# An expert layer of eight equal steps becomes four full experts beside four half-empty ones

## The chip, the core and the metric

The program runs on one core of a Trainium2 chip. The metric is the device time of one execution in microseconds (us); the kernel before takes 1585.5 us (median of three runs, 1585.26 to 1587.52).

## The reference, cut to what matters

Two decoder layers over 256 tokens of width 1024. Each has three token mixers, a merge and a LayerNorm; then layer 0 has a dense SwiGLU and layer 1, with which this case deals, eight experts of which each token takes two:

```
logits = x @ w_router                                   # 256 x 8
top_logit, top_idx = top_k(logits, 2); top_w = softmax(top_logit)
for each expert e, its tokens xs:
    y = (silu(xs @ w_gate[e]) * (xs @ w_up[e])) @ w_down[e]     # 1024 -> 2816 -> 1024
out[token] += top_w * y;   x = LayerNorm(alpha * x + out)
```

All is float32. The inputs are fixed (seed 0). The weights of the eight experts are 8 x 3 x 1024 x 2816 x 4 bytes = 276.8 MB and are read once.

## The kernel before

Every weight travels in units of 1 MB (128 partitions x 2048 float32), in the order in which `pack` laid them down. `fetch` (L166) has SyncE (SP) start the transfer of the next unit into the next of seven buffers of the expert layer (six `raw`, one `ga`); a buffer is free when both its halves have been split. `split` (L188) turns half a unit, 128x1024, into `hi` (rounded to fp32r, ScalarE, ACT, L196) and `lo` (the rest, VectorE, DVE, L198), in one of nine pairs of buffers. `mm3` (L206) then makes a product of nearly float32 precision from three TensorE (PE) matmuls: activation-high by hi, activation-high by lo, activation-low by hi (L208 to L210).

Expert layer (`moe`, L1031): a step is 256 of the 2816 inner columns of one expert, three units: two of gate and up, one of down. There are 8 experts x 11 = 88 steps, expert after expert in the order of memory. An expert has 128 slots; `gather` makes a one-hot matrix from the tokens' places and multiplies, so that the slots' activations stand as `xeh` (high) and `xel` (low), 128 columns each, for two experts at once. Per step, PE does 24 matmuls of 512 columns for gate and up into the PSUM tile `pa`, then ACT (Silu, L1093) and DVE (times up, L1094) make the hidden activation, PE transposes it (L1099), ACT and DVE split it into `hh` and `hl` (L1103, L1104), and PE does 12 matmuls for down, one step later (`pend`), into two tiles `Y`. After an expert's last step `scatter` splits Y, multiplies with the turned one-hots `oht` (L1056, L1057) and adds the weighted rows into the accumulator `ybc` (L221). `weights` (L963) makes the softmax weights and the fullest expert's count.

Should an expert have more than 128 tokens, `spill` (L1117) does the rest in a loop that reads all weights again, with addresses from a register; the trace shows only its test (TENSOR_LOAD of `mosti`, L1119).

A scheduler orders each engine's instructions, from the program's order and its own estimate of readiness; `issue_after` holds single ones back. Each engine executes its own list in order and waits on semaphores.

Of the kernel before, what the change touches and what calls it, by code (L numbers as in the profile page):

```python
# [21 lines left out]
T = 256  # L22
# [4 lines left out]
NE = 8  # L27
# [18 lines left out]
GA = 3  # L46
# [88 lines left out]
class Net:  # L135
# [29 lines left out]
    def fetch(self):  # L165
# [5 lines left out]
        w = self.A["wst"][self.unit]  # L171
# [742 lines left out]
    def route_consts(self):  # L914
# [12 lines left out]
        nc.vector.tensor_copy(self.identr, self.ident)  # L927
        self.sel = C.tile([128, 2, NE], F32, name="sel")
# [34 lines left out]
    def weights(self):  # L963
        nc, C = self.nc, self.cst
        ps = self.pa()
        for m in range(2):
            nc.tensor.matmul(ps[:, 0:NE], lhsT=self.ones, rhs=self.sel[:, m], start=m == 0, stop=m == 1)
        most = C.tile([128, 1], F32, name="most")
        nc.vector.tensor_reduce(most, ps[:, 0:NE], axis=AX.X, op=OP.max)
        self.most = C.tile([128, 1], I32, name="mosti")  # L970
        nc.vector.tensor_copy(self.most, most)
# [7 lines left out]
        for m in range(2):  # L979
            nc.vector.tensor_scalar(ex[:, m], ex[:, m], den[:, m:m + 1], None, op0=OP.mult)  # L980
            nc.vector.tensor_scalar(self.wt[:, m], self.oh8[:, m, 0], ex[:, m, 0:1], None, op0=OP.mult)
            self.stt(self.wt[:, m], self.oh8[:, m, 1], ex[:, m, 1:2], self.wt[:, m])
        self.dump("pos", self.pos)
        self.dump("wt", self.wt)

    def gather(self, es, W):
        nc = self.nc
        n = len(es)
        oh = W.tile([128, 2, n * 128], F32R, name="ohm", bufs=2)
        self.front = []  # L990
        for m in range(2):
            for i, e in enumerate(es):
                self.front.append(nc.vector.tensor_scalar(oh[:, m, i * 128:(i + 1) * 128], self.slot,
                                                          self.pos[:, m, e:e + 1], None, op0=OP.is_equal))
        xeh = [W.tile([128, 8, 128], F32R, name="xeh", bufs=3) for _ in es]
        xel = [W.tile([128, 8, 128], F32R, name="xel", bufs=3) for _ in es]
        for kp in range(4):
            ps = self.pa()
            for kk in range(2):
                k = 2 * kp + kk  # L1000
                s = slice(k * 128, (k + 1) * 128)
                o = ps[:, kk * 256:kk * 256 + n * 128]
                for m in range(2):
                    nc.tensor.matmul(o, lhsT=self.xkh[:, m, s], rhs=oh[:, m], start=m == 0, stop=False)  # L1004
                    nc.tensor.matmul(o, lhsT=self.xkl[:, m, s], rhs=oh[:, m], start=False, stop=m == 1)
            pv = ps.rearrange("p (k i t) -> p k i t", k=2, t=128)
            for i in range(n):
                q = slice(2 * kp, 2 * kp + 2)
                nc.scalar.copy(xeh[i][:, q], pv[:, :, i])
                self.front.append(nc.vector.tensor_sub(xel[i][:, q], pv[:, :, i], xeh[i][:, q]))  # L1010
            yield
        return [xeh, xel, oh]

    def finish(self, gen):
        while True:
            try:
                next(gen)
            except StopIteration as r:
                return r.value

    def turn(self, oh, W):
        nc = self.nc
        oht = W.tile([128, 2, T], F32R, name="oht", bufs=2)
        for i in range(2):
            ps = self.psA.tile([128, 512], F32R, name="pa")
            for m in range(2):
                nc.tensor.transpose(ps[:, m * 128:(m + 1) * 128], oh[:, m, i * 128:(i + 1) * 128], self.identr)
            nc.scalar.copy(oht[:, i], ps[:, 0:T])  # L1028
        return oht

    def moe(self, W):  # L1031
        nc = self.nc
        acc = self.macc
        got = coming = None
# [3 lines left out]
        pend = None  # L1038

        def down(j, hh, hl2, wd, Y, ns=(0, 1)):  # L1040
            for f in range(2):
                for n in ns:
                    s = slice(n * 512, (n + 1) * 512)
                    self.mm3(Y[n], hh[:, f], hl2[:, f], wd[f][0][:, s], wd[f][1][:, s], j == 0 and f == 0,
                             j == NJ - 1 and f == 1)

        def scatter(e, Y, oht, ns=(0, 1)):
            for n in ns:
# [3 lines left out]
                nc.scalar.copy(yh, Y[n])  # L1052
                nc.vector.tensor_sub(yl, Y[n], yh)
                for m in range(2):
                    ps = self.pb()
                    nc.tensor.matmul(ps, lhsT=oht[:, m * 128:(m + 1) * 128], rhs=yh, start=True, stop=False)  # L1056
                    nc.tensor.matmul(ps, lhsT=oht[:, m * 128:(m + 1) * 128], rhs=yl, start=False, stop=True)  # L1057
                    self.stt(acc[:, m, s], ps, self.wt[:, m, e:e + 1], acc[:, m, s])

        for e in range(NE):  # L1060
            if e % 2 == 0:
                got = self.finish(coming or self.gather((e, e + 1), W))
                coming = None
                if e == 0:
                    self.after(SPLITS[1], self.front[SPLITS[4]])
            Y = oht = None
            for j in range(NJ):
                if e == 0 and j == 1:
                    self.weights()
                    for m in range(2):  # L1070
                        nc.scalar.mul(acc[:, m], self.xt[m], ALPHA)
                if e % 2 and e < NE - 1 and GA <= j < GA + 4:
                    if coming is None:
                        coming = self.gather((e + 1, e + 2), W)
                    next(coming, None)
                if j == 2:
                    if e % 2 == 0:
                        got[2] = self.turn(got[2], W)
                    oht = got[2][:, e % 2]
                ps = self.pa()  # L1080
                for u in range(2):
                    raw = self.fetch()
                    for h in range(2):
                        hi, lo = self.split(raw[:, h * 1024:(h + 1) * 1024])
                        for kk in range(2):
                            k = 4 * u + 2 * h + kk
                            s = slice(kk * 512, (kk + 1) * 512)
                            self.mm3(ps, got[0][e % 2][:, k], got[1][e % 2][:, k], hi[:, s], lo[:, s], k == 0, k == 7)
                        if u == 1 and h == 0 and pend is not None and not (e == NE - 1 and j == NJ - 1):
                            pend()  # L1090
                            pend = None
                sg = W.tile([128, 256], F32, name="fs", bufs=2)
                nc.scalar.activation(sg, ps[:, 0:256], AF.Silu)  # L1093
                nc.vector.tensor_mul(sg, sg, ps[:, 256:512])  # L1094
                wd = list(self.halves())
                last = e == NE - 1 and j == NJ - 1
                pt = self.pb()
                for f in range(2):
                    nc.tensor.transpose(pt[:, f * 128:(f + 1) * 128], sg[:, f * 128:(f + 1) * 128], self.ident)  # L1099
                hh = W.tile([128, 2, 128], F32R, name="hh", bufs=2)  # L1100
                hl2 = W.tile([128, 2, 128], F32R, name="hl2", bufs=2)
                pv = pt[:, 0:256].rearrange("p (a t) -> p a t", a=2)
                nc.scalar.copy(hh, pv)  # L1103
                nc.vector.tensor_sub(hl2, pv, hh)  # L1104
                if Y is None:
                    Y = [self.pb(), self.pb()]
                before = pend

                def pend(ns=(0, 1), j=j, hh=hh, hl2=hl2, wd=wd, Y=Y, e=e, oht=oht):
                    down(j, hh, hl2, wd, Y, ns)  # L1110
                    if j == NJ - 1:
                        scatter(e, Y, oht, ns)
        for n in range(2):
            before((n,))
            pend((n,))

    def spill(self, W, base, after):  # L1117
# [10 lines left out]
        oht = W.tile([128, T], F32, name="oht", bufs=2)  # L1128
# [5 lines left out]
        with tc.If(most > 128):  # L1134
            nc.vector.tensor_scalar(pos, self.pos, -128.0, None, op0=OP.add)
# [142 lines left out]
```

## Time and profile before

| what | us |
|---|---|
| median of three runs | 1585.5 |
| the profiled execution | 1585.51 |
| its span (first to last instruction) | 1583.7 |
| PE / DVE / ACT busy in it | 1518.6 / 1275.1 / 931.7 |
| moved by DMA | 390.78 MB, 247 GB/s over the span |

The profile's page gives the busy time of each engine and cuts the span into 40 slices of 39.6 us; the expert layer is slices 20 to 40. The views of the trace used below are the busy time, granted clock and DMA rate of a stretch (windows), the instructions of a stretch in order of time (timeline), groups of equal instructions (lines), the events of one line of the source, and DMA issues.

### The profile page before, as it was taken

What the parts mean: (1) busy time and instruction counts of PE and PEld (TensorE: products, weight loads), DVE (VectorE), ACT (ScalarE), POOL (GpSimd) and SP (SyncE); (2) the same over time, 40 slices, a digit from 0 to 9 for tenths busy, and PEclk for the clock granted to TensorE, in tenths of its full rate; (3) what the DMA queues carried; (4) which work ended last, traced back from release to release, by engine and by line L of the source; (5) the groups of instructions that cost most, each with busy time, mean ns of one, the idle gap of its engine ahead of it and who ended that gap; (6) DMA issues with size and microseconds to landing.
All of it is one profiled execution on the core that took longest, in us unless ns stands there. A gap on an engine that the chain in (4) does not pass through costs nothing.

```text
span 1583.7 us, 23704 instructions
## 1 busy us (share of the span) xinstructions
PE 1518.6 (96%) x9398; PEld 1312.9 (83%) x9398; DVE 1275.1 (81%) x1717; ACT 931.7 (59%) x1235; POOL 44.4 (3%) x80
## 2 busy tenths in 40 slices
PE   7999999999999989999899999999999999999996
PEld 7989987999989989998788887887878878788784
DVE  6899588654556898578898988889898888888887
ACT  6433454544436433454777777777777767777673
POOL 1030000000000110000000000000000000000000
PEclk9999999999999999999899999999999999999998
DMA  6343246655414343245698898998989988899892
GB/s 230 110 160 131 94 152 234 218 208 186 173 67 147 107 146 121 94 179 233 263 353 349 329 351 307 369 359 317 349 318 366 363 331 332 321 360 363 330 372 76
DMA packets 55637, 390.78 MB, mean 247 GB/s; under 512 B 6192, under 2 KB 6192, under 8 KB 9568
## 3 DMA queue, kind: packets, MB, share of 16 engines
q1 hardware_dynamic: 53136, 381.18, 63.8%
q0 software_dynamic: 2096, 7.49, 1.4%
q8 instruction: 76, 1.25, 0.3%
q10 hardware_dynamic: 288, 0.52, 0.1%
q14 instruction: 41, 0.34, 0.1%
HBM read 387.08 MB, written 2.10 MB: 246 GB/s over the span
## 4 chain that ended last, share of the span: by engine, by line
PE 89%; DVE 7%; ACT 2%; issue 1%; DMA 0%; DVEq 0%; ACTq 0%; POOLq 0%
PE pa L208 19%; PE pa L209 19%; PE pa L210 19%; PE pb L208 7%; PE pb L210 7%; PE pb L209 7%; PE pb L585 2%; DVE lo L198 2%; PE pb L1099 1%; DVE ga L221 1%; ACT hi L196 1%; DVE M L523 1%; PE pa L1004 1%; DVE r L563 1%; DVE kk L540 1%
## 5 line engine op out<-in xcount | busy, mean ns | idle before, releaser
L198 DVE TENSOR_TENSOR lo<-raw,hi 128x1024 fp32r<-128x1024 f32 x648 | 771.2, 1223 | 149.4 <-ACT hi L196 146.9
L196 ACT CAST hi<-raw 128x1024 fp32r<-128x1024 f32 x648 | 655.8, 1050 | 281.7 <-PE pa L209 192.3
L208 PE MATMUL pa<-xTh,hi 128*128 128x256 f32 x1120 | 325.4, 291 | 7.3 <-ACT xTh L347 7.3
L210 PE MATMUL pa<-xTh,lo 128*128 128x256 f32 x1120 | 323.2, 289 | 7.0 <-DVE lo L198 6.8
L209 PE MATMUL pa<-xTl,hi 128*128 128x256 f32 x1120 | 321.7, 287 | 2.3 <-DVE xTl L348 2.0
L210 PE MATMUL pa<-hi,xel 128*128 128x512 f32 x704 | 283.1, 402 | 0.0
L208 PE MATMUL pa<-hi,xeh 128*128 128x512 f32 x704 | 279.9, 398 | 0.4 <-ACT oht L1028 0.4
L209 PE MATMUL pa<-lo,xeh 128*128 128x512 f32 x704 | 279.3, 397 | 0.0
L208 PEld LDWEIGHTS pa<-xTh,hi 128*128 128x128 f32 x1120 | 218.5, 195 | 12.0 <-ACT xTh L347 7.3
L210 PEld LDWEIGHTS pa<-xTh,lo 128*128 128x128 f32 x1120 | 218.6, 195 | 10.3 <-DVE lo L198 8.8
L209 PEld LDWEIGHTS pa<-xTl,hi 128*128 128x128 f32 x1120 | 218.6, 195 | 3.6 <-DVE xTl L348 2.3
L208 PE MATMUL pb<-hi,hh 128*128 128x512 f32 x440 | 174.4, 396 | 3.7 <-ACT hh L1103 3.7
L209 PE MATMUL pb<-lo,hh 128*128 128x512 f32 x440 | 173.4, 394 | 0.0
L210 PE MATMUL pb<-hi,hl 128*128 128x512 f32 x440 | 173.3, 395 | 0.0
L209 PEld LDWEIGHTS pa<-lo,xeh 128*128 128x128 f32 x704 | 132.6, 188 | 30.5
L210 PEld LDWEIGHTS pa<-hi,xel 128*128 128x128 f32 x704 | 132.6, 188 | 29.0
L208 PEld LDWEIGHTS pa<-hi,xeh 128*128 128x128 f32 x704 | 132.8, 189 | 28.6 <-ACT oht L1028 0.6
L1093 ACT ACTIVATE fs<-pa 128x256 f32<-128x256 f32 x88 | 33.9, 385 | 150.9 <-PE pa L210 150.9
L208 PEld LDWEIGHTS pb<-hi,hh 128*128 128x128 f32 x440 | 82.6, 188 | 24.2 <-ACT hh L1103 5.3
L210 PEld LDWEIGHTS pb<-hi,hl 128*128 128x128 f32 x440 | 82.6, 188 | 19.9 <-DVE hl L1104 0.2
L209 PEld LDWEIGHTS pb<-lo,hh 128*128 128x128 f32 x440 | 82.6, 188 | 19.3
L198 DVE TENSOR_TENSOR lo<-ga,hi 128x1024 fp32r<-128x1024 f32 x74 | 88.0, 1218 | 5.1 <-ACT hi L196 4.8
(329 smaller groups left out, 1538.4 us busy)
## 6 DMA issues: line engine op xcount, KB each, us to landing
raw<-in_wst SPq DMA_DIRECT2D x322, 1024.0 KB, 6.0
ga<-in_wst SPq DMA_DIRECT2D x37, 1024.0 KB, 6.8
raw<-in_wst SPq DMA_DIRECT2D x4, 512.0 KB, 5.8
xf<-in_xT SPq DMA_DIRECT2D x2, 512.0 KB, 5.5
raw<-in_lora SPq DMA_DIRECT2D x2, 512.0 KB, 5.7
kk<-in_lnp POOLq DMA_DIRECT2D x2, 512.0 KB, 3.9
v<-in_lnp POOLq DMA_DIRECT2D x2, 512.0 KB, 3.9
xsave<-ga POOLq DMA_DIRECT2D x2, 512.0 KB, 2.9
```

The source lines that it names most:

```text
L196: self.nc.scalar.copy(hi, src)
L198: self.nc.vector.tensor_sub(lo, src, hi)
L208: mm(out, lhsT=lh, rhs=rh, start=start, stop=False)
L209: mm(out, lhsT=lh, rhs=rl, start=False, stop=False)
L210: mm(out, lhsT=ll, rhs=rh, start=False, stop=stop)
L221: return self.nc.vector.scalar_tensor_tensor(out, a, s, b, op0=op0, op1=op1)
L523: nc.vector.tensor_mul(M[:, c % 2, c // 2, 4 * hb:4 * hb + 4], ps.rearrange("p (a t) -> p a t", a=4), self.mask[:, None, :].to_broadcast([ ...
L540: nc.vector.transpose(y[32 * q:32 * q + 32], src)
L563: self.inv = nc.vector.transpose(o, E[s].rearrange("p t b s -> p t (b s)"))
L585: ins = nc.tensor.matmul(ps[s, n * 64:(n + 1) * 64], lhsT=lhsT[s, 8 * b + n], rhs=rhs[s, 8 * b + n], start=True, stop=True)
L1004: nc.tensor.matmul(o, lhsT=self.xkh[:, m, s], rhs=oh[:, m], start=m == 0, stop=False)
L1093: nc.scalar.activation(sg, ps[:, 0:256], AF.Silu)
```

## The change

The number of tokens of each expert is now used. `rank` orders the experts by count on DVE: `order` (which expert has rank r), `posr` and `wtr` (places and weights by rank) and `cap` (128 for ranks 0 to 3, 64 for ranks 4 to 7); rank 0 is always expert 0 (its `tie` is 8192), whatever its count, the ranks behind it go by count. Ranks 0 to 3 ("big") are done as before, three passes on 128 slots. Ranks 4 to 7 ("small") have 64 slots: `xes` holds the 64 high and the 64 low columns side by side as one operand of 128, and `mm2` makes two matmuls, with hi and with lo, where `mm3` makes three. Gate and up then stand in two partial sums, one in rows 0 to 63 and one in 64 to 127; ACT copies them out (`gu`) and four matmuls with `fold` (two identities on top of each other) add and transpose them. The partial sums of down are added by the scatter, whose one-hots stand twice (`slot2`).

Steps alternate: two big ones, then small, big, small, big to the end, and the down product of a step stands two steps (`LAG`) behind its gate and up. Units of ranks 1 to 7 are read at an address in a register: SP loads seven entries of `order` first. Within the layer the scheduler is off for PE, DVE, ACT and SP: what stands where is given by the program, by lags counted in halves of units (`at`). `spill` now starts above the caps.

The diff, cut to its core:

```diff
-GA = 3
+BIG = 4
+LIMITS = 128, 64
+LAG = 2
...
-    def weights(self):
+    def weights(self, W):
...
-        nc.vector.tensor_reduce(most, ps[:, 0:NE], axis=AX.X, op=OP.max)
...
+        nc.vector.tensor_copy(cnt, ps[:, 0:NE])
+        self.rank(cnt, W)
...
+    def expert_unit(self, r, j, c):
+        if r == 0:
+            return self.A["wst"][self.base + 3 * j + c]
+        if not self.who:
+            for i in range(1, NE):
+                self.who[i] = self.nc.values_load(self.order[0:1, i:i + 1], engines=(mybir.EngineType.SP,),
+                                                  min_val=0, max_val=NE - 1)
+        src = self.A["wst"][bass.ds(self.who[r] * (3 * NJ) + (self.base + 3 * j + c), 1)]
+        return src.rearrange("a p c -> p (a c)")
...
+        steps = [streams[0].pop(0) for _ in range(2)]
+        while streams[0] or streams[1]:
+            for st in (streams[1], streams[0]):
+                if st:
+                    steps.append(st.pop(0))
+        halves = []
+        for i in range(len(steps) + LAG):
+            if i < len(steps):
+                halves += [(0, steps[i], h) for h in range(4)]
+            if i >= LAG:
+                halves += [(1, steps[i - LAG], f) for f in range(2)]
...
+        def hidden_small(r, j, ps):
+            gu = W.tile([128, 512], F32, name="gu")
+            nc.scalar.copy(gu, ps)
+            pt = self.pa()
+            for f in range(4):
+                nc.tensor.matmul(pt[:, f * 64:(f + 1) * 64], lhsT=gu[:, f * 128:(f + 1) * 128], rhs=self.fold,
+                                 start=True, stop=True)
...
+            def act():
+                sg = W.tile([128, 2, 64], F32, name="fs", bufs=2)
+                nc.scalar.activation(sg, pv[:, 0:2], AF.Silu)
+                nc.vector.tensor_mul(sg, sg, pv[:, 2:4])
+
+                def split():
+                    hh = W.tile([128, 2, 128], F32R, name="hh", bufs=2)
+                    nc.scalar.copy(hh[:, :, 0:64], sg)
+                    nc.vector.tensor_sub(hh[:, :, 64:128], sg, hh[:, :, 0:64])
...
+            for now, (kind, rj, i) in enumerate(halves):
+                if i % 2 == 0:
+                    raw = self.fetch(self.expert_unit(*rj, 2 if kind else i // 2))
+                h = i % 2
+                hl = self.split(raw[:, h * 1024:(h + 1) * 1024])
+                product(kind, rj, i, hl)
+                if now == 0:
+                    at(1, lambda: self.weights(W))
...
+                due(now)
...
+    def mm2(self, out, l, rh, rl, start, stop):
+        self.nc.tensor.matmul(out, lhsT=l, rhs=rh, start=start, stop=False)
+        self.nc.tensor.matmul(out, lhsT=l, rhs=rl, start=False, stop=stop)
```

Before, DVE stood like this at the start of the layer (`xel`: low part of the gathered activations, `lo`: low half of weights, `den`, `ex`, `wt`: softmax weights):

```order
L198 TENSOR_TENSOR lo<-raw,hi 128x1024 x2
L1010 TENSOR_TENSOR xel<-pa,xeh 128x256 x2
L977 TENSOR_TENSOR den<-ex 128x2
L198 TENSOR_TENSOR lo<-raw,hi 128x1024
L1010 TENSOR_TENSOR xel<-pa,xeh 128x256 x3
L978 RECIPROCAL den<-den 128x2
L198 TENSOR_TENSOR lo<-raw,hi 128x1024
L1010 TENSOR_TENSOR xel<-pa,xeh 128x256 x2
L980 TENSOR_SCALAR ex<-ex,den 128x2 x2
```

Now the gather's rows stand together, and behind them all of `weights` and `rank`, 30 instructions in 27 rows from `cnt` to `wtr`, of which the first rows are:

```order
L1081 TENSOR_TENSOR xel<-pa,xeh 128x256 x4
L981 COPY cnt<-pb 128x8
L223 SCALAR_TENSOR_TENSOR key<-cnt,tie 128x8
L1004 TENSOR_TENSOR fs<-key 128x64
L1007 TENSOR_REDUCE rk<-fs 128x8
L1009 TENSOR_TENSOR perm<-rk,io_7346 128x64
L1011 TENSOR_TENSOR fs<-perm,io_7346 128x64
L1013 TENSOR_REDUCE of<-fs 128x8
L1015 CAST order<-of 128x8
```

No `lo` stands between them any more: the third half of the layer is split behind the 30, and `cnt` waits for a matmul that stands on PE behind the first two halves' products.

Before, PE did a step in the middle of the layer like this (`ident,fs`: the transposes of the hidden activation; `pa`: gate and up; `pb`: down):

```order
L208 MATMUL pa<-hi,xeh 128x512
L209 MATMUL pa<-lo,xeh 128x512
L1099 MATMUL pb<-ident,fs 128x128 x2
L210 MATMUL pa<-hi,xel 128x512
...
L208 MATMUL pb<-hi,hh 128x512
L209 MATMUL pb<-lo,hh 128x512
L210 MATMUL pb<-hi,hl_11431 128x512
```

Now a big step, with the fold of the small step ahead of it, is followed by a small one, with the transposes of the big one:

```order
L212 MATMUL pa<-hi,xel 128x512
L1193 MATMUL pa<-fold,gu 128x64 x4
...
L1298 MATMUL pa<-hi,xes 128x512
L1299 MATMUL pa<-lo,xes 128x512
L1176 MATMUL pa<-ident,fs 128x128 x2
...
L1298 MATMUL pb<-hi,hh 128x512
L1299 MATMUL pb<-lo,hh 128x512
```

A small step has 16 and 8 long matmuls where a big one has 24 and 12, and nothing of one half of a unit stands ahead of the half before it.

## Rows read from the trace of the kernel before

**Rows 1.** The page: span, busy times, a group's idle time before it.
```profile
span 1583.7 us, 23704 instructions
...
PE 1518.6 (96%) x9398; PEld 1312.9 (83%) x9398; DVE 1275.1 (81%) x1717; ACT 931.7 (59%) x1235; POOL 44.4 (3%) x80
...
L1093 ACT ACTIVATE fs<-pa 128x256 f32<-128x256 f32 x88 | 33.9, 385 | 150.9 <-PE pa L210 150.9
```

**Rows 2.** Windows: stretch, busy of PE, PEld, DVE, ACT, POOL; clock, DMA share, GB/s.
```profile
760.00:777.00 17.00, 15.15 (x70) 13.03 (x69) 14.76 (x31) 10.99 (x17) 0.00 (x0) 0.82 0.75 285
800.00:1555.00 755.00, 744.65 (x3324) 598.27 (x3323) 671.00 (x732) 547.62 (x705) 1.05 (x2) 1.00 0.89 342
840.00:860.00 20.00, 20.00 (x89) 16.09 (x88) 18.27 (x19) 15.83 (x18) 0.00 (x0) 1.00 1.01 414
980.00:1000.00 20.00, 20.00 (x89) 16.09 (x89) 19.06 (x23) 13.09 (x16) 0.00 (x0) 1.00 0.99 372
1440.00:1460.00 20.00, 20.00 (x90) 16.07 (x90) 17.86 (x19) 15.43 (x21) 0.00 (x0) 1.00 0.98 353
```

**Rows 3.** Timeline of DVE, two steps: start, us, instruction [idle before, ended by].
```profile
1202.78 0.42 DVE L1094 TENSOR_TENSOR fs<-fs,pa 128x256 f32<-128x256 f32 x1 [0.45 <-ACT fs L1093]
1203.71 2.36 DVE L198 TENSOR_TENSOR lo<-raw,hi 128x1024 fp32r<-128x1024 f32 x2 [0.52 <-ACT hi L196]
1205.99 0.42 DVE L1104 TENSOR_TENSOR hl<-pb,hh 128x256 fp32r<-128x256 f32 x1
1206.33 2.35 DVE L198 TENSOR_TENSOR lo<-ga,hi 128x1024 fp32r<-128x1024 f32 x2
...
1211.39 0.42 DVE L1094 TENSOR_TENSOR fs<-fs,pa 128x256 f32<-128x256 f32 x1 [0.44 <-ACT fs L1093]
...
1214.94 4.62 DVE L198 TENSOR_TENSOR lo<-raw,hi 128x1024 fp32r<-128x1024 f32 x4
```

**Rows 4.** Timeline of PE, the same stretch.
```profile
1200.76 0.39 PE L208 MATMUL pa<-hi,xeh 128*128 128x512 f32 x1
1200.99 0.39 PE L209 MATMUL pa<-lo,xeh 128*128 128x512 f32 x1
...
1204.02 0.38 PE L1099 MATMUL pb<-ident,fs 128*128 128x128 f32 x2
```

**Rows 5.** Lines by form, PE, before the layer: group, count, busy, mean ns.
```profile
L663 PE MATMUL pb<-QR,Sbd 128*128 128x64 f32 x48 | 6.6, 281 | 0.0
```

**Rows 6.** Timeline of DVE, an expert's end.
```profile
969.90 1.28 DVE L1053 TENSOR_TENSOR yl<-pb,yh 128x512 fp32r<-128x512 f32 x2
971.89 2.73 DVE L221 SCALAR_TENSOR_TENSOR ybc<-pb,wt,ybc 128x512 f32<-128x512 f32 x4 [0.72 <-PE pb L1057]
```

**Rows 7.** Timeline of DVE, start of the layer: small instructions.
```profile
758.57 0.47 DVE L993 TENSOR_SCALAR ohm<-slot,pos 128x128 fp32r<-128x128 f32 x2
765.00 1.08 DVE L1010 TENSOR_TENSOR xel<-pa,xeh 128x256 fp32r<-128x256 f32 x3
768.03 0.35 DVE L980 TENSOR_SCALAR ex<-ex,den 128x2 f32<-128x2 f32 x2
```

**Rows 8.** Timeline of PE, start of the layer.
```profile
767.05 0.63 PE L208 MATMUL pa<-hi,xeh 128*128 128x512 f32 x1
767.48 0.63 PE L209 MATMUL pa<-lo,xeh 128*128 128x512 f32 x1
...
770.70 0.40 PE L210 MATMUL pa<-hi,xel 128*128 128x512 f32 x1
```

**Rows 9.** Source line L1119: duration ns min/median/max, start.
```profile
L1119 SPq TENSOR_LOAD <-mosti x1: 483/483/483, 1542.6 to 1542.6; - x1
L1119 SPq FUSED_REGOPS  x1: 186/186/186, 1543.1 to 1543.1; - x1
```

**Rows 10.** DMA issues, 740 to 800 us: count, size, median us to landing.
```profile
raw<-in_wst SPq DMA_DIRECT2D x12, 1024.0 KB, 4.8
```

**Rows 11.** Timeline of DVE, the end.
```profile
1569.74 1.41 DVE L221 SCALAR_TENSOR_TENSOR ybc<-pb,wt,ybc 128x512 f32<-128x512 f32 x2
```

More of the change, by code (lines that the diff above doesn't have):

```diff
@@ L170, in fetch @@
         raw = pool.tile([128, 2048], F32, name=name)
-        w = self.A["wst"][self.unit]
+        w = self.A["wst"][self.unit] if src is None else src
         if self.unit in CUT:
@@ L1002, in gather @@
-                o = ps[:, kk * 256:kk * 256 + n * 128]
+                s = slice((2 * kp + kk) * 128, (2 * kp + kk + 1) * 128)
+                o = ps[:, kk * w:(kk + 1) * w]
                 for m in range(2):
[L1004 to L1029, printed above, removed]
+                    nc.tensor.matmul(o, lhsT=self.xkh[:, m, s], rhs=oh[:, m, a:b], start=m == 0, stop=False)
@@ L1037, in moe @@
         self.cycle = [order[(i - u) % (n + 1)] for i in range(n + 1)]
[L1038 to L1048, printed above, removed]
+        self.base, self.who = u, {}
@@ new lines, in coming, with go, pe @@
+        def coming(big, small, lag, gap):
+            def go():
+                oh, _ = self.one_hots(big, small, W)
+                xb, xs, mms, highs, lows = self.gather(oh, big is not None, small is not None, W)
+                if big is not None:
+                    xe[big], ohs[big] = xb, (oh, 0)
+                if small is not None:
+                    xe[small], ohs[small] = xs, (oh, 128)
+                for kp in range(4):
+                    def pe(kp=kp):
+                        pv = mms(kp, self.pb)
+                        at(4, lambda: highs(pv, kp))
+                        at(4, lambda: lows(pv, kp))
+                    at(1 + gap * kp, pe)
+                for i, r in enumerate((big, small)):
+                    if r is not None:
+                        turn(r, 4 * gap + 2 + 2 * i)
+            at(lag, go)
@@ L1049, in scatter, with half @@
+        def scatter(r, quick=False):
+            y = Y.pop(r)
+            d = 0 if quick else 1
+            def half(n):
                 s = slice(n * 512, (n + 1) * 512)
@@ L1060, in moe @@
[L1060 to L1069, printed above, removed]
-                    for m in range(2):
[L1071 to L1112, printed above, removed]
@@ new lines, in half, with product @@
+                for m in range(2):
+                    at(d * (1 + 2 * m), lambda m=m: mm(m))
+            at(4 * d, lambda: half(0))
+            at(6 * d, lambda: half(1))
+        def product(kind, rj, i, hl):
+            r, j = rj
+            big = r < BIG
+            hi, lo = hl
+            if kind == 0:
+                if i == 0:
+                    gps[rj] = self.pa()
+                ps = gps[rj]
+                for kk in range(2):
+                    k, s = 2 * i + kk, slice(kk * 512, (kk + 1) * 512)
+                    if big:
+                        self.mm3(ps, xe[r][0][:, k], xe[r][1][:, k], hi[:, s], lo[:, s], k == 0, k == 7)
+                    else:
+                        self.mm2(ps, xe[r][:, k], hi[:, s], lo[:, s], k == 0, k == 7)
+                if i == 3:
+                    del gps[rj]
+                    at(4, lambda: (hidden_big if big else hidden_small)(r, j, ps))
+            else:
+                while rj not in hid:
+                    x = min(later)
+                    later.remove(x)
+                    x[2]()
+                if r not in Y:
+                    Y[r] = [self.pb(), self.pb()]
+                for n in range(2):
+                    s = slice(n * 512, (n + 1) * 512)
+                    first, last = j == 0 and i == 0, j == NJ - 1 and i == 1
+                    h = hid[rj]
+                    if big:
+                        self.mm3(Y[r][n], h[0][:, i], h[1][:, i], hi[:, s], lo[:, s], first, last)
+                    else:
+                        self.mm2(Y[r][n], h[0][:, i], hi[:, s], lo[:, s], first, last)
+                if i == 1:
+                    del hid[rj]
+                    if j == NJ - 1:
+                        scatter(r, quick=now > len(halves) - 8)
```

194 lines of the change are left out of this document (162 added, 32 removed).

## The prediction

> **What bounds the kernel now.** I read the page first, then windows over the expert layer, then timelines of single steps on DVE and PE, and last the transfers. The page has PE busy for 1518.6 of 1583.7 us [rows 1], and from 800 to 1555 us for 744.65 of 755 at a granted clock of 1.00 (the level of 2.4 GHz), with DVE busy for 671.0 and the DMA engines for 0.89 of the time [rows 2]. That PE sets the pace, and is not merely busy, shows on DVE: in each step it idles 0.45 us until ACT's Silu, which itself waits for gate and up on PE (150.9 us of idle time before 88 of them [rows 1]), and then 0.52 us for the next `hi` [rows 3], while PE starts a long matmul every 0.233 us without a gap [rows 4]. A step takes 1211.39 - 1202.78 = 8.61 us [rows 3], and 36 matmuls by 0.233 and the two transposes make that up. So less PE work shortens a step, until the next resource ends last. The question is which one, and it is close: DVE and DMA were at nine tenths already.
>
> **PE, what goes.** A small step has 24 long matmuls instead of 36 and four fold matmuls instead of two transposes. The fold's shape (128x64, float32, 128 by 128 weights) is in the trace: 48 of them took 6.6 us, 0.14 each [rows 5]. A small step thus costs 24 x 0.233 + 4 x 0.14 = 6.15 us and a pair of steps 8.61 + 6.15 = 14.76. All 44 pairs take 649 us; scatters (8 x 8 matmuls by 0.233 = 15) and gathers (160 matmuls of 64 to 192 columns, by columns about 0.07 of the 0.233 us that 512 take; 11) make 675.
>
> **DVE, what stays.** Every half unit is still split, and `lo` back to back costs (4.62 - 2.36) / 2 = 1.13 us [rows 3]. A big step keeps L1094 and L1104, each 0.34 us in a row of others (1205.99 to 1206.33). In a small one both are half as wide; no row has that width from PSUM, so I take 0.2 from the 128x128 rows, 0.47 us for two, and bound it by 0.15 and 0.34 [rows 7]; the bounds move the sum by -4 and +12 us. An expert's end costs 1.28 + 2.73 = 4.0 us [rows 6], eight of them 32. From the third half on (below) there are 526 halves: 526 x 1.13 = 594; 44 x 0.68 = 30; 44 x 0.4 = 18; scatter 32; gathers and one-hots 12 x 0.33 + 30 x 0.2 = 10. The sum is 684 us, or 15.5 per pair: more than PE's 675.
>
> **DMA, what stays.** The bytes are the same, 264 units of 1.0486 MB. In the whole stretch the engines moved 342 GB/s at a share of 0.89 [rows 2], so at a full share 342 / 0.89 = 384 GB/s, 2.73 us a unit, 16.4 per pair. That is longer than PE's 14.8 and DVE's 15.5. It isn't a fixed price: the best stretch had 414 GB/s at 1.01 (2.53 us) and the worst 353 at 0.98 (360 at a full share, 2.91 us) [rows 2], with the same work on all engines; 372 at 0.99 lies between. I take 2.73, the mean of the long row.
>
> The Trainium skill, HBM Reference, section Specifications (TRN2), gives a core that streams alone about 425 GB/s and a core whose neighbour streams too about 358. By the first a unit would take an estimated 2.47 us and the time would be that of the rival "DVE"; by the second 2.93 us and that of the rival "slow memory". The rows lie on both sides of neither and settle between them.
>
> **The start.** Before, the first product starts at 767.05 us and the 12 of the first two halves end near 770.9; meanwhile DVE goes on splitting [rows 8]. Now the first gather is half as wide, so I put the first product at 764 (between 763 and 767), its twelfth matmul at 768. There `cnt` waits for its matmul, and behind it stand the 30 small instructions with no split between: 0.175 us each when independent [rows 7], 0.2 with the waits on each other, 6 us, and some 0.5 for the exponential on ACT. Queued behind them is the split of the third half, so DVE resumes splitting at 775 and PE gets its thirteenth product near 776.5, 5.5 us later than before (bounds 3 and 10). The clock in this stretch is 0.82 [rows 2], and matmuls start 0.43 us apart until it rises [rows 8]; PE's new gap may keep it low some us longer, which costs little since DVE then leads.
>
> On SP four units of rank 0 can start early, as against seven before; the fifth waits for `order`, the eighth of the 30 (near 770), and for seven register loads. One costs 0.483 + 0.186 and some 0.1 between [rows 9], seven 5.5 us: the first transfer goes out at 775.5 and lands 4.8 us later [rows 10], at 780.3. DVE wants it at 775 + 6 x 1.13 + about 1 = 782.8, so this wait is just covered; if the loads cost 1.2 us each it would show by a microsecond.
>
> A transfer with its address in a register does not occur in the trace. SP's part can be bounded by the address computation, 0.19 us [rows 9], added to a plain issue, and above by a transfer that is issued only when the one ahead has landed, 4.8 us a unit [rows 10]. I take the lower: it needs no other resource than SP, which has 2.7 us per unit.
>
> **In-order lists.** With no scheduler a wait of one instruction holds all behind it. I followed a pair through the lags. The tightest place is the small step's Silu on ACT, three halves behind the fold: product and fold of the second half of a big step end some 2.3 us after its `lo`, Silu and the next `hi` take 1.4 more, and DVE needs that `hi` after 3 x 1.13 + 0.2 = 3.6 us: 0.1 us of waiting per pair. All others have half a microsecond or more. Expected cost: 5 us in all, hidden while DMA is last.
>
> **The sum.** The 260 register-addressed units land from 780.3 on, the last at 780.3 + 259 x 2.73 = 1487.4. Now and then the ring of seven is full while DVE does scatters and gathers (42 us in all, mostly absorbed by buffers): I add a quarter, 10 us, 1497. After the last landing come a split (1.2), four products (0.9), `yh`, `yl`, the scatter's matmuls and four adds (0.6 + 1.3 + 0.5 + 2.7 [rows 6]): 7.2. From the end of the last add to the end of the span it was 1583.7 - 1571.15 = 12.5 us [rows 1, 11], and that stays. The span becomes 1516.7; the profiled execution took 1585.51, 1.8 more than its span and the same as the median of 1585.5. Forecast: 1518 us, 67 faster. Of 44 x 2.46 = 108 us of PE work that go, 67 are gained, and the rest is lost to the transfers, which end last instead. Its own range, from 2.65 to 2.82 us a unit, is 1497 to 1542.
>
> **Rivals.**
> *DVE decides.* If the unit takes 2.55 us as in the best stretch, the last lands at 1441 and DVE ends last: 775 + 684 = 1459, with 2% of waits as PE has now 1473, then 12.5 + 1.8: 1487 us. For it speaks that stretch, against it that only the first part of the layer shows such rates.
>
> *Slow memory.* At 2.91 us a unit, as in the worst stretch [rows 2]: 780.3 + 754 + 19.7 + 1.8 = 1556, 1560 with some ring loss. For it speaks that the windows late in the layer lie at 353 to 372 GB/s with the engines busy for 0.98 to 0.99; against, the mean.
>
> *The waits stay.* If DVE keeps the 0.45 + 0.52 us of idle time per step [rows 3], now from in-order lists, DVE's 684 become 769 and the time is 775 + 769 + 14.3 = 1558.
>
> *Register addresses slow the transfers: the slower side.* Place: SP's queue. Price: whatever lengthens the unit. From 780.3 + 259 t + 21.5 = 1585.5 follows t = 3.03 us; above it the kernel is slower than before, and with one transfer at a time (4.8) it takes 2045 us. For it: no row shows such a transfer in a stream. Against it: a transfer lasts 4.8 us and one starts every 3.07 now [rows 2, 10], so they overlap, and nothing in the list makes one wait for another's landing.
>
> *It doesn't do what it says.* If a small expert had more than 64 tokens the loop over all experts would run, which reads the weights again, with thousands of microseconds. The inputs are fixed, and the reference's formulas give 119, 107, 68, 61, 52, 52, 27 and 26 tokens; expert 0, always big, has 52. So it doesn't run.
>
> **Chances.** Forecast 0.48, DVE 0.18, slow memory 0.16, waits 0.10, register addresses 0.06, spill or something unseen 0.02. The first four are faster by more than 0.2% (about what a measurement here can tell from no change), with a little of the slower ones near the break-even: faster 0.91, same 0.02, slower 0.07. The range is 1484 to 1562: it takes in DVE's 1487 and slow memory's 1560 and leaves out the tails and the slower side.
>
> **What would show it.** In the profile after, from 800 us on: DMA share 0.96 or more; PE busy under 0.95; DVE idle before `lo` with ACT's `hi`, and that with a landing, as the releaser; issue to landing near 7 us instead of 4.8. A small step's PE work 6.15 us, a pair 16 to 16.5 us long. At the start one block of small DVE instructions of 6 to 7 us with PE idle beside it, and seven loads on SP of 0.8 us each. Wrong it would be if a pair took 15.5 us with DVE full (DVE decides), if DVE idled behind Silu or `gu` with data landed (waits), or if the DMA engines idled while SP issues (register addresses).

## The result, and the profile after

The changed kernel takes 1520.6 us (median of four runs, 1520.3 to 1524.7) against 1586.3 for the kernel before beside it: ratio 0.959, 95% interval 0.957 to 0.961, 66 us faster. The forecast was 1518. The time came right; what ends last did not. The page (span, busy times, DMA issues with count, size and median us to landing):

```profile
span 1518.5 us, 23759 instructions
...
PE 1442.1 (95%) x9166; PEld 1250.2 (82%) x9166; DVE 1256.2 (83%) x1740; ACT 933.3 (61%) x1279; POOL 44.3 (3%) x80
...
raw<-in_wst SPq DMA_DIRECT2D x322, 1024.0 KB, 6.9
```

Windows, columns as in [rows 2]: the start, the layer, a stretch of plain pairs, and four pairs in which one pair of experts ends and the next is gathered.

```profile
760.00:777.00 17.00, 10.62 (x39) 8.97 (x38) 7.87 (x35) 6.11 (x10) 0.00 (x0) 0.60 0.00 0
...
800.00:1490.00 690.00, 675.92 (x3136) 541.42 (x3134) 663.03 (x751) 564.50 (x766) 1.05 (x2) 1.00 0.95 384
...
1220.00:1300.00 80.00, 80.00 (x372) 65.24 (x371) 78.74 (x86) 68.07 (x90) 0.00 (x0) 1.00 1.01 416
...
943.58:1019.46 75.88, 71.14 (x330) 55.03 (x330) 70.03 (x89) 56.01 (x81) 0.00 (x0) 1.00 0.87 340
```

At the start nothing is transferred, where [rows 2] had 285 GB/s, and PE is busy for 10.6 of 17 us. In plain pairs everything looks full: PE 80.00 of 80, DVE 78.74, DMA share 1.01. No single row of these says which one ends last. DVE's timeline of one such pair answers to [rows 3]:

```profile
1276.81 0.28 DVE L1200 TENSOR_TENSOR fs<-fs,pa 128x128 f32<-128x128 f32 x1
1277.33 2.36 DVE L200 TENSOR_TENSOR lo<-raw,hi 128x1024 fp32r<-128x1024 f32 x2 [0.25 <-ACT hi L198]
1279.61 0.28 DVE L1205 TENSOR_TENSOR hh<-fs,hh 128x128 fp32r<-128x128 f32 x1
1279.81 1.22 DVE L200 TENSOR_TENSOR lo<-raw,hi 128x1024 fp32r<-128x1024 f32 x1
1280.95 0.41 DVE L1171 TENSOR_TENSOR fs<-fs,pa 128x256 f32<-128x256 f32 x1
1281.28 4.62 DVE L200 TENSOR_TENSOR lo<-raw,hi 128x1024 fp32r<-128x1024 f32 x4
...
1291.91 0.28 DVE L1200 TENSOR_TENSOR fs<-fs,pa 128x128 f32<-128x128 f32 x1
```

From one small step's `fs` to the next, which is a pair of one small and one big step, it is 1291.91 - 1276.81 = 15.10 us. DVE has one wait of 0.25 in it, and that for a `hi`. ACT, which makes `hi`, itself waits for PE there and never for a landing; these are all its waits between 1220 and 1310 us (us in total, times, longest):

```profile
ACT hh L1182 <- PE pa L1176: 7.7, 6, 1.3
ACT fs L1199 <- PE pa L1193: 5.0, 6, 0.8
```

30 of the 43 such intervals lie between 15.05 and 15.3 us; a pair in which no expert begins or ends is called plain below.

PE in the same pair, answering to [rows 4] and [rows 5]:

```profile
1284.34 0.38 PE L1176 MATMUL pa<-ident,fs 128*128 128x128 f32 x2
...
1289.93 0.40 PE L212 MATMUL pa<-hi,xel 128*128 128x512 f32 x1
1290.16 1.00 PE L1193 MATMUL pa<-fold,gu 128*128 128x64 f32 x8
1290.97 0.48 PE L210 MATMUL pa<-hi,xeh 128*128 128x512 f32 x1
1291.29 0.40 PE L211 MATMUL pa<-lo,xeh 128*128 128x512 f32 x1
```

A fold is eight rows, not four, and takes 0.81 us to the next matmul's start and 0.09 more behind it, 0.90 in all. PE has no gap: 60 long matmuls by 0.233, 0.90, and two transposes with 0.22 make its pair 15.1.

The other 13 intervals, and one of 15.29, hold the rest of the layer: the first two pairs, the last, and the three changes. These changes of experts take four, four and three pairs: 20.81 + 16.07 + 21.94 + 17.06 = 75.88 us twice and 56.0 once, 15.5, 15.5 and 10.7 more than plain pairs. DVE's waits in the first:

```profile
DVE ybc L223 <- PE pb L1224: 4.6, 4, 1.5
DVE lo L200 <- ACT hi L198: 0.8, 2, 0.5
DVE hl L1183 <- ACT hh L1182: 0.5, 1, 0.5
```

At the start, DVE's timeline; it answers to [rows 7]:

```profile
769.87 0.17 DVE L981 COPY cnt<-pb 128x8 f32<-128x8 f32 x1 [4.35 <-PE pb L979]
...
771.55 0.17 DVE L1015 CAST order<-of 128x8 int32<-128x8 f32 x1
...
776.02 0.29 DVE L1033 TENSOR_REDUCE wtr<-fs 128x16 f32<-128x128 f32 x1
776.23 1.21 DVE L200 TENSOR_TENSOR lo<-raw,hi 128x1024 fp32r<-128x1024 f32 x1
```

And the end, which answers to [rows 11]:

```profile
1484.07 1.22 DVE L200 TENSOR_TENSOR lo<-raw,hi 128x1024 fp32r<-128x1024 f32 x1
1486.99 1.39 DVE L1219 TENSOR_TENSOR yl<-pb,yh 128x512 fp32r<-128x512 f32 x2 [1.70 <-ACT yh L1218]
...
1497.26 0.29 DVE L1200 TENSOR_TENSOR fs<-fs,pa 128x128 f32<-128x128 f32 x1 [2.65 <-ACT fs L1199]
...
1502.63 2.73 DVE L223 SCALAR_TENSOR_TENSOR ybc<-pb,wtr,ybc 128x512 f32<-128x512 f32 x4
```

The last unit is issued by 1474 (two parts, about 6 us to landing), so the data are there near 1480; the last add ends at 1505.4. At the end, too, the data wait for compute.

### The profile page after: what moved, and what is told of

Its sections match the earlier page's. It is cut to its first block, busy times and chain, and to the rows that moved or that the text cites. A ratio compares the mean times of both kernels' runs of the same rounds, so it can differ in the third digit from the quotient of the medians.

```text
span 1518.5 us, 23759 instructions
## 1 busy us (share of the span) xinstructions
PE 1442.1 (95%) x9166; PEld 1250.2 (82%) x9166; DVE 1256.2 (83%) x1740; ACT 933.3 (61%) x1279; POOL 44.3 (3%) x80
## 4 chain that ended last, share of the span: by engine, by line
PE 82%; DVE 14%; issue 2%; ACT 2%; DMA 0%; DVEq 0%; ACTq 0%; POOLq 0%
PE pa L211 14%; PE pa L210 14%; PE pa L212 14%; DVE lo L200 6%; PE pa L1299 4%; PE pb L212 4%; PE pb L210 4%; PE pb L211 4%; PE pa L1298 4%; PE pa L1193 2%; PE pb L1299 2%; PE pb L1298 2%; PE pb L587 2%; DVE ga L223 1%; DVE ybc L223 1%
## 5 line engine op out<-in xcount | busy, mean ns | idle before, releaser
L210 PE MATMUL pa<-hi,xeh 128*128 128x512 f32 x352 | 145.2, 413 | 5.0 <-ACT hi L198 5.0
L211 PE MATMUL pa<-lo,xeh 128*128 128x512 f32 x352 | 142.6, 405 | 6.6 <-DVE lo L200 6.6
L1299 PE MATMUL pa<-lo,xes 128*128 128x512 f32 x352 | 140.4, 399 | 6.1 <-DVE lo L200 6.1
L1298 PE MATMUL pa<-hi,xes 128*128 128x512 f32 x352 | 143.2, 407 | 0.0
L212 PE MATMUL pa<-hi,xel 128*128 128x512 f32 x352 | 140.7, 400 | 0.0
L211 PE MATMUL pb<-lo,hh 128*128 128x512 f32 x264 | 104.6, 396 | 1.0 <-DVE lo L200 1.0
L210 PE MATMUL pb<-hi,hh 128*128 128x512 f32 x264 | 104.6, 396 | 0.0
L212 PE MATMUL pb<-hi,hl 128*128 128x512 f32 x264 | 104.3, 395 | 0.0
L1299 PEld LDWEIGHTS pa<-lo,xes 128*128 128x128 f32 x352 | 66.3, 188 | 24.6 <-DVE lo L200 11.4
L1298 PEld LDWEIGHTS pa<-hi,xes 128*128 128x128 f32 x352 | 66.2, 188 | 13.0
```

What stands on the lines that cost most here:

```text
L210: mm(out, lhsT=lh, rhs=rh, start=start, stop=False)
L211: mm(out, lhsT=lh, rhs=rl, start=False, stop=False)
L212: mm(out, lhsT=ll, rhs=rh, start=False, stop=stop)
L1298: self.nc.tensor.matmul(out, lhsT=l, rhs=rh, start=start, stop=False)
L1299: self.nc.tensor.matmul(out, lhsT=l, rhs=rl, start=False, stop=stop)
```

## The experiments

Each kernel is the changed one (1520.6) with the edit shown. The times are medians of four executions, the ratios are to the kernel before, and the quoted text was written before the run. Theory T is the forecast's: the transfers end last. P, later called B, says that compute ends last: PE, with DVE and the waits between the engines' lists close behind it.

**Half the bytes for the small experts.**

```diff
+        elif part:
+            self.nc.sync.dma_start(raw[:, 0:1024], w[:, 0:1024])
...
-                    raw = self.fetch(self.expert_unit(*rj, 2 if kind else i // 2))
-                h = i % 2
+                    raw = self.fetch(self.expert_unit(*rj, 2 if kind else i // 2), rj[0] >= BIG)
+                h = i % 2 if rj[0] < BIG else 0
```

> Left out: of each unit of the small experts only the first half is fetched, and both halves of the split use it; the work of PE, DVE and ACT is the same. Theory T (the forecast's: the transfers end last): in the profile after, a pair of steps takes 15.10 us in 36 of 43 pairs, 2.52 us a unit; with a quarter of the bytes gone a pair falls to what PE and DVE were put at, 14.8: 44 x 0.3 = 13 us less, 1507 or below. Theory P (PE still ends last: its pair is 15.1 and not 14.76, since it idles nowhere in these pairs): the pair stays at 15.10 and the time at 1520 within 4 us, with the DMA share near 0.75.

1520.4 us (ratio 0.958, 0.957 to 0.960): nothing changed. (The plain pairs are 30, not 36 as written there.) The window of plain pairs, against the one above:

```profile
1220.00:1300.00 80.00, 80.00 (x371) 65.19 (x371) 78.73 (x85) 68.03 (x90) 0.00 (x0) 1.00 0.85 309
```

Share 0.85 instead of 1.01, 309 GB/s instead of 416, the same pair of 15.10. T falls: the share of 1.01 did not mean that the transfers end last. They are close behind all the same, as the run without low halves will show: 14.91 us for the six units of a pair, against 15.10.

**Less work on PE.**

```diff
-                        self.mm2(Y[r][n], h[0][:, i], hi[:, s], lo[:, s], first, last)
+                        nc.tensor.matmul(Y[r][n], lhsT=h[0][:, i], rhs=hi[:, s], start=first, stop=last)
```

> Left out: the products of down with the low half of the weights for the small experts (4 of the 24 long matmuls of a small step, 0.93 us of PE per pair); DVE, ACT and the transfers are the same. T: pair 15.10, time 1520 within 4 us. P: PE's pair falls to 14.2, so DVE ends last, 12 x 1.13 + 0.67 + 0.4 = 14.65 and at most 0.25 of waits: pair 14.65 to 14.9, 36 x 0.2 to 0.45 = 7 to 16 us less, 1504 to 1513. If P is right but the transfers come next, the pair stops between 14.9 and 15.1.

1518.7 us (0.957, 0.956 to 0.959); pair 15.04. PE now waits for `lo` between 1220 and 1310 us:

```profile
PE pa L211 <- DVE lo L200: 3.6, 6, 0.6
```

So PE had been last, but by 0.06 us only. The next limit is not DVE's bare work as P had it, since a wait of 0.2 for `hi` stays in each pair. P's number was missed.

**Both edits at once.**

> Both edits at once: half the bytes for the small experts and 4 long matmuls less per pair. T: as with half the bytes alone, 1507 or below. P with DVE next: as with less PE work alone, pair 14.65 to 14.9, 1504 to 1513. P with the transfers next: clearly faster than with less PE work alone.

1521.7 us (0.959, 0.957 to 0.961), pair 15.04. No difference from the two alone: the transfers were not what stopped the kernel with less PE work either.

**The alternation undone.**

```diff
-        while streams[0] or streams[1]:
-            for st in (streams[1], streams[0]):
-                if st:
-                    steps.append(st.pop(0))
+        steps += streams[0] + streams[1]
...
-                if kind == 0 and i == 0 and j == 2 and 0 < r + 1 < BIG:
-                    coming(r + 1, r + 1 + BIG, 1, 6)
+                if kind == 0 and i == 0 and j == 2 and r + 1 < NE:
+                    coming(*((r + 1, None) if r + 1 < BIG else (None, r + 1)), 1, 6)
```

> The alternation is undone: 44 big steps, then 44 small ones, each small expert gathered one expert ahead; the same work. With P a big step takes PE's 8.61 us and a small one what ends last there without PE (6.3): DVE's 6 x 1.13 + 0.4 = 7.2 or the transfers' 3 x 2.5 = 7.5. A pair then costs 15.8 to 16.1 instead of 15.1: 44 x 0.7 to 1.0 = 31 to 44 us more, less some 5 at the start, where the order of the experts is wanted later: 1547 to 1560. With T at the forecast's 2.73 us a small step takes 8.2 and a pair 16.8: 1565 or more.

1544.9 us (0.973, 0.972 to 0.975): 24 slower, a little under the range. A plain big step takes 8.62 us with PE full, a small one 7.21 with DVE full (no wait in its timeline): 15.83 a pair, the 0.73 expected, 32 us for 44. The rest of the layer gave back 8, where some 5 had been expected at the start; a reason may be that gathers and scatters of big experts now stand beside steps in which DVE has room, but no run shows it. Alternating is worth 24 us here.

**No low half of down for the small experts.**

```diff
+                hl = self.split(raw[:, h * 1024:(h + 1) * 1024], not kind or rj[0] < BIG)
...
-                        self.mm2(Y[r][n], h[0][:, i], hi[:, s], lo[:, s], first, last)
+                        nc.tensor.matmul(Y[r][n], lhsT=h[0][:, i], rhs=hi[:, s], start=first, stop=last)
```

> Left out: the low half of the weights of down for the small experts, its split on DVE (2 of 12 in a pair) and its products on PE (4 of 60 long matmuls). Theory B (in a pair PE with 15.10 and DVE with 15.04 end almost together, the transfers have room): DVE falls to 12.8, PE to 14.2, so the pair becomes 14.2, 36 x 0.9 = 32 us less in the plain pairs and some 6 at the experts' changes: 1478 to 1486. Rival M (the transfers come right behind, at the 2.50 us a unit that they have at share 1.01): pair 15.0, 1513 to 1517. In between, the pair divided by 6 is the price of a unit when the transfers end last.

1501.4 us (0.948, 0.944 to 0.951), neither range; the gain is at the changes and at the end, while the plain pair stays at 15.01. That looks like the rival M, at 419 GB/s. But DVE's waits between 1220 and 1310 us name something else:

```profile
DVE hl L1185 <- ACT hh L1184: 7.6, 5, 1.5
DVE lo L202 <- ACT hi L198: 3.6, 11, 0.5
```

DVE waits for `hh`, which waits on ACT for PE's transposes, and PE waits for the `lo` that stands behind `hl` on DVE (4.1 us, six times): a loop through three in-order lists. The run that follows tells it from M.

**The same, with more room in the lists.**

```diff
-                at(3, split)
+                at(4, split)
...
-            at(3, act)
+            at(4, act)
```

> As the run without the low half of down for the small experts, and the split of the hidden activation of a big step and the Silu of a small one each stand one half later in the lists. In that run the pair was 15.01 us with PE's work at 14.2, DVE's at 12.8 and the transfers at a share of 1.01. Theory L (a loop through the in-order lists: transposes on PE, hh on ACT, hl on DVE, and behind them the hi and lo for which PE waits): one half more is 1.1 us of room, the pair falls to PE's 14.2, 36 x 0.8 = 29 us less than 1501: 1470 to 1478. Theory M (transfers at 2.50 us a unit): 15.0 stays, 1498 to 1505.

1468.9 us (0.926, 0.925 to 0.928): 32 less for two lags, pair 14.17, which is PE's work. The loop was the cause. ACT's waits between 1220 and 1310 us now have a landing among them, 0.5 us in all: at 14.17 / 6 = 2.36 us a unit compute asks for a little more than the transfers give in the run that follows, and the difference can only come out of the ring, filled at the changes. Little more is to be had here without fewer bytes: all 43 intervals of this run average 14.94 us, and with the transfers alone, in that run, a pair takes 14.91.

**No low halves at all: the transfers by themselves.**

```diff
+                hl = self.split(raw[:, h * 1024:(h + 1) * 1024], False)
...
-                        self.mm3(ps, xe[r][0][:, k], xe[r][1][:, k], hi[:, s], lo[:, s], k == 0, k == 7)
+                    nc.tensor.matmul(ps, lhsT=x[:, k], rhs=hi[:, s], start=k == 0, stop=k == 7)
```

> Left out: all low halves of the expert layer's weights and the products with them and with the low activations, so that a half unit is one hi on ACT and one matmul pass on PE, and the transfers have nothing of compute in their way but ACT's 12 x 0.95 + 1.5 = 12.9 us a pair (PE 8.1). The forecast's unit of 2.73 us: pair 16.4, 1545 to 1560. A unit of 2.50 (419 GB/s, the best stretches): pair 15.0, about 1490. ACT last: pair 12.9, about 1395. Whatever the pair is, if hi waits for landings a sixth of it is what a unit costs when transfers do end last.

1462.2 us (0.921, 0.920 to 0.923); pair 14.91 almost throughout, so a unit costs 2.485 us. Here the transfers do end last, and this is how that looks. The window:

```profile
1220.00:1300.00 80.00, 63.33 (x197) 36.97 (x196) 15.69 (x33) 72.42 (x95) 0.00 (x0) 0.81 1.01 421
```

The page's DMA issues, and ACT's waits between 1220 and 1310 us:

```profile
raw<-in_wst SPq DMA_DIRECT2D x322, 1024.0 KB, 15.1
```

```profile
ACT hi L198 <- DMA raw<-in_wst: 7.3, 18, 0.7
ACT hi L198 <- DMA ga<-in_wst: 1.0, 3, 0.5
```

The share is 1.01 as in the changed kernel. What differs is that `hi` waits for landings, and that it is 15.1 us from issue to landing (six units in flight) instead of 6.9. The total was expected near 1490: with so little compute, the changes and the end cost next to nothing.

**Scatter adds three halves behind their matmul.**

```diff
-                    at(d, lambda: self.stt(acc[:, m, s], ps, self.wtr[:, m, r:r + 1], acc[:, m, s]))
+                    at(SCAT * d, lambda: self.stt(acc[:, m, s], ps, self.wtr[:, m, r:r + 1], acc[:, m, s]))
```

with `SCAT = 3`.

> The adds of a scatter stand three halves behind their matmul on DVE instead of one, nothing else. In the profile after, DVE waits at each of the three changes of experts 0.8 to 1.5 us four times for the scatter's matmul, 4.5 in all. Theory W (DVE ends last there, and these waits are paid in full): 3 x 4.5 = 13 us less, 1505 to 1510. Rival (PE or the burst of DVE's work decides there, or the waits come back as waits for banks of PSUM): 1517 to 1522.

1507.5 us (0.950, 0.947 to 0.954), 13 less as W had it. A change goes from 75.88 to 18.19 + 16.73 + 18.98 + 17.06 = 70.96 us: 4.9 less, and no wait of DVE for the scatter is left in it.

**Four big steps first, the small instructions spread out.**

```diff
-        steps = [streams[0].pop(0) for _ in range(2)]
+        steps = [streams[0].pop(0) for _ in range(4)]
...
-                    at(1, lambda: self.weights(W))
+                    small = self.weights(W)
+                    at(1, lambda: next(small))
+                    for k in range(3, 3+(32+2-1)//2):
+                        at(k, lambda: [next(small, None) for _ in range(2)])
...
-                    coming(None, BIG, 2, 1)
+                    coming(None, BIG, 8, 2)
```

`weights` and what it calls yield after each DVE instruction.

> Four big steps stand ahead of the first small one instead of two, and the 30 small DVE instructions are spread by two over the halves from the third on; gathers of the next experts two steps later. The first ten units are then of rank 0, and no transfer waits for the order. Theory B (compute ends last from the start on): the block of 6.4 us on DVE goes into steps in which PE leads by 1.1 us each, 4 us gained; the waits of the first gather (the first two pairs are 17.4 and 17.0 instead of 15.1) 4 more; two steps more that do not alternate cost 1.5: 1512 to 1516. Theory T (a transfer not started costs its time at the end): the 40 us without transfers are worth three buffers, 3 x 2.5 = 7.5 us more than that: 1504 to 1508.

1510.5 us (0.952, 0.949 to 0.955): 10 less, between the two ranges. It does not tell them apart; the run with half the bytes already has. Nor did the gain come as B had it: the first two pairs nearly keep their length (16.95 and 17.04 us), so the 4 us expected from them were not gained. The start gained about 8 instead of 4: the first small `fs` is at 812.25 us instead of 803.35, with two more big steps (17.2 us) ahead of it.

**One split in twelve on GpSimd.**

```diff
+                hl = self.split(raw[:, h * 1024:(h + 1) * 1024], nc.gpsimd if now > 20 and now % 12 in (6,) else None)
...
-            self.nc.vector.tensor_sub(lo, src, hi)
+            (eng or self.nc.vector).tensor_sub(lo, src, hi)
```

> One of the twelve splits of a pair has its low half made by GpSimd instead of DVE. DVE's pair falls to 13.9. Theory B: PE's 15.10 stays for the plain pairs, 36 x 0.05 at most; at the experts' changes, 75.9 us for four pairs, DVE has 4.5 less to do and the rest comes near PE's 66.8: 3 x 6 to 9 = 18 to 27 us less, 1493 to 1502. Rival (the two engines hold each other up): where a GpSimd split holds DVE for as long as it lasts, 2 to 4 us a pair, the pair becomes 16 to 18 and the time 1555 to 1640.

1535.3 us (0.969, 0.965 to 0.972), 15 slower; pair 15.56. A split on GpSimd, in its timeline:

```profile
1221.93 3.00 POOL L200 TENSOR_TENSOR lo<-raw,hi 128x1024 fp32r<-128x1024 f32 x1 [12.57 <-ACT hi L198]
```

And the one that DVE makes beside it:

```profile
1224.26 1.75 DVE L200 TENSOR_TENSOR lo<-raw,hi 128x1024 fp32r<-128x1024 f32 x1 [0.65 <-ACT hi L198]
```

GpSimd takes 3.0 us, and DVE's split beside it 1.75 instead of 1.22; why, no run shows. DVE isn't held for as long as GpSimd's split lasts: its `fs` of 0.29 us at 1223.32 stands in the middle of it. So the rival is right in sign, not in size. The pair of 15.56 can be read from the trace in part. PE's work is 15.10 as before, and in each pair it comes 0.47 us late for one `lo`: its matmuls at 1234.29 and 1234.88 are 0.59 apart instead of 0.233, and the next is 0.11 late. From 1224.26 up to that `lo` DVE works without a wait. What makes it late stands at the start: a wait of 0.66 for the Silu that follows the fold on PE, one of 0.65 for the `hi` behind that Silu, and the slow split. By its looks that is a loop through the lists again; later lags were not tried with this edit.

**Late scatter adds and the other start together.**

> Two edits together that were run apart: the adds of a scatter three halves behind their matmul (13 us less alone), and four big steps first with the small instructions of the order spread out (10 us less alone). They lie in different places, the changes of experts and the start, so if compute ends last throughout the gains add: 1497, between 1494 and 1501. If a resource with no room is behind both (transfers at 2.50 us a unit, 264 units from 740 on, would allow it, so nothing here asks for this), the second gives less than half: above 1502.

1497.5 us (0.944, 0.943 to 0.946): the gains add, as far as an interval of 2 to 3 us can tell. It computes all that the changed kernel does, in 23 us less. From 800 to 1460 us PE is busy for 654.65 of 660 and DVE for 648.25.

**And with the lags of the lists and a fold of single passes.**

```diff
-            gu = W.tile([128, 512], F32, name="gu")
+            gu = W.tile([128, 512], F32R, name="gu")
...
-        self.fold = C.tile([128, 64], F32, name="fold")
+        self.fold = C.tile([128, 64], F32R, name="fold")
```

> The two edits together once more (1497), and with them the later split and Silu, and the fold in fp32r: gate and up of a small expert are rounded to fp32r before the fold adds them, so that each of its four matmuls is one pass on PE instead of two. The trace has eight passes of 0.10 us in a fold. If a pass less saves that, PE's pair falls from 15.10 to 14.7, and DVE's own work, 14.85 with no wait left in it, ends last: 35 pairs by 0.2 to 0.25 and 2 at the changes, 7 to 11 us less: 1486 to 1490. If the fold's cost is its weight loads or the lists hold both engines up as before: 1494 to 1499. Transfers at 14.9 a pair, as where all low halves were left out, would stop it at the same place as DVE.

1479.8 us (0.932, 0.929 to 0.935), 18 less where 7 to 11 were expected. The pair is 14.69 and DVE has no wait at all in it; the fold has half the rows. The window, and a fold in PE's timeline:

```profile
1220.00:1300.00 80.00, 79.63 (x357) 63.48 (x357) 80.00 (x90) 69.56 (x92) 0.00 (x0) 1.00 1.01 415
```

```profile
1222.17 0.53 PE L1217 MATMUL pa<-fold,gu 128*128 128x64 f32 x4
```

So DVE's bare work in a pair is 14.69, 0.16 less than the 14.85 that had still held small waits. Lags and fold were not run apart here; in the run with less PE work, without the later lags, the pair fell by 0.06 only, which speaks for the lags being needed for the rest.

## Why the prediction was right, and where it was not

**Right as forecast: what a step costs DVE, and the start.** DVE's pair, put at 12 x 1.13 + 0.68 + 0.4 = 14.64, measures 14.69 in the last run, where it has no waits; the narrow instructions take the 0.2 they were put at. First product 764.5 (764), the block of 30 instructions 769.87 to 776.23 = 6.4 us (6.5), first transfer with a register address at 776.2 (775.5); the seven loads took 4.1 us (5.5), one every 0.6. The quicker loads made up for `order`, which came at 771.7, not near 770. Addresses from registers cost nothing that shows: these transfers reach 416 GB/s, and with little of compute in their way 421. That rival falls. The list that was called the tightest, the small step's Silu, is the one place where DVE waits in a plain pair: 0.25 us, put at 0.1.

**Wrong: "transfers, which end last instead".** This is the step that failed. The unit was put at 342 / 0.89 = 2.73 us, as if a share of 1 at the mean rate were the limit. The run without low halves gives 2.485. With that the forecast's own sum is 780.3 + 259 x 2.485 = 1424 for the last landing, not 1487, so other resources decide. Measured in the kernel itself, a quarter of the bytes away moved the time by nothing. The long window's 342 GB/s was the pace of PE, which ended last then, and a share of 0.89 is no measure of how much more would go. Of the marks that the prediction set, the share (0.95 over all, 1.01 in plain pairs) and the latency (6.9 us) came as forecast and did not show what they were meant to. The latency could not: the 4.8 us it was set against are from 740 to 800 us, and in the layer of the kernel before it was 6.7 already (median of 208 units, 800 to 1555 us), with PE last. The three marks that could tell came out against it: PE busy 0.98, not under 0.95; the pair 15.10, not 16 to 16.5; no `hi` waiting for a landing. The Trainium skill, HBM Reference, section Specifications (TRN2), gives a core that streams alone about 425 GB/s, where these runs have 421; it stood for the rival "DVE", and the measurement agrees with it.

**Wrong: PE's fold.** The group [rows 5] counts 48, and the loop at L663 makes 24 matmuls of that kind (three chunks, four each, in two layers), so a float32 matmul is two rows; I took a row for a matmul. Four of them cost 0.90 us, not 0.56, and PE's pair is 15.1 instead of 14.76: 44 x 0.34 = 15 us. This put PE 0.06 us above what came next, the waits between the lists, and kept it last in the plain pairs. (A gather's matmul was too cheap as well: eight of them take 0.87 us on PE, 0.11 each, not 0.07.) The rival "DVE" is so half right: DVE is close behind PE there (14.69 against 15.10), and last at the changes.

**Wrong: scatters and gathers "mostly absorbed by buffers".** Their DVE work was summed over the layer (42 us, 10 of them counted). But two experts end and two are gathered within four pairs. DVE is busy for 70.0 of 75.9 us there and waits 4.6 for scatter matmuls: behind their matmul by one half, the adds had too little room in the list, although all places but the Silu's were given half a microsecond or more. The run with late adds gave that back. The three changes cost 42 us over plain pairs.

**Why the time came right all the same.** The forecast had 259 units by 2.73 us, 707, and 10 for the ring up to the last landing, and 7.2 from there to the last add. The plain pace is 15.10 / 6 = 2.52 us a unit, 652 for 259 units, 55 less. The three changes add 42 to that and the first two pairs, in which PE, without a gap, also does a gather's matmuls, 4 (17.4 and 17.0 us): 36 more than the ring's 10; and from the last landing, near 1480, to the last add it is 25 us, 18 more, since the data wait for compute. So -55 stands against 36 and 18. These errors have nothing to do with each other; that they cancel is luck. From the last add to the end of the span it is 1518.5 - 1505.4 = 13.1 us (12.5).

**What stays open:** why a split on DVE is slower beside one on GpSimd, whether later lags would make that edit pay, and how much of the last run's 18 us belongs to the lags and how much to the fold.

## What to carry to other kernels

With a prefetch ring, a DMA share near 1.0 does not say that the transfers end last: it was 1.01 here both when they did and when they did not. Look whether their consumer waits for a landing and whether the time to landing grows towards the whole ring (15.1 us here, against 6.9); leaving out bytes tells it in one run. Where three engines lie within 3% of each other, sum what each has in the densest stretch and not over the layer, and follow each loop that closes through in-order lists (a wait on one engine that delays, over the lists of others, what this engine itself waits for next). Adds that stand two halves later were worth 13 us at the changes, and two instructions one half later 32 in a kernel whose engines all had room. Count the rows that one instruction of the program makes before a duration is multiplied.

## What was not expected of the hardware

A float32 matmul of 64 columns stands in the trace as two rows, 0.10 us apart; rounded to fp32r it is one row, and the fold's PE time halves. In the run without low halves the DMA engines held 421 GB/s at a share of 1.01 from 800 to 1400 us. A subtraction of 128x1024 takes GpSimd 3.0 us and DVE 1.22, and 1.75 on DVE beside GpSimd's.
